# Attention's stores on GpSimd's queue, fewer loads for the scan, and the block solve in four half slots

## The chip, the cores and the metric

The kernel runs on one core of one Trainium2 chip. The metric is device time in microseconds (us) of one execution. The engines are named as the profile names them: PE (TensorE, the matmuls), PEld (its weight loads), DVE (VectorE), ACT (ScalarE), POOL (GpSimd) and SP (SyncE, which here only issues DMAs). A "queue" is the list of DMAs that one engine issues: SPq, ACTq, POOLq. An engine issues its own DMAs in its own instruction stream, so a DMA that has to wait holds up what stands behind it on that engine.

## The reference

One inference step of a two-layer hybrid backbone, for 128 context tokens and 1024 latent tokens of width 1024. In every layer the modulated input goes through one input projection whose columns feed three heads side by side; their outputs are joined, projected and normalised, and a gated feed-forward part follows:

```
z_rw, zq, zkv, zkr, zu, zv = split_proj(x * (1 + scale1) + shift1, w_in, rw_conv)
y_rw, s_fin = rwkv7_bidir(z_rw, s0)     # 4 heads of 64, forward and backward over the tokens:
      S = S * w_t + (S @ -kk_t) (kk_t * a_t)^T + v_t k_t^T ;  out_t = S @ r_t
y_mla = attend(...)                     # 8 heads: softmax(scale * (q_nope k_nope + q_rope k_rope)) @ v,
                                        # 1024 latent queries over 1152 keys, 128 context queries over 128
y_gm  = chunk_mlp(zu, zv)
x = layer_norm(ALPHA * x + gate1 * (concat(y_rw, y_mla, y_gm) @ w_out))
x = layer_norm(ALPHA * x + gate2 * swiglu(x * (1 + scale2) + shift2))
```

All of it is float32 in and out. The outputs are the two token streams, the compressed attention caches and the final scan states of the context.

## The kernel before

**Stages.** Each layer runs the input projection, the preparation of attention's q, k and v (written to DRAM as `qd`, `kd`, `vd`) and of the scan's inputs (decays `sd`, columns `zd`, values `vtd`), then one stage in which attention and the RWKV scan are woven together, then `w_out` and the feed-forward part. A matmul of float32 accuracy is written as three products of split operands, lines L119 to L121. Only the woven stage matters here. It runs in layer 0 from about 365 to 920 us and in layer 1 from about 2250 to 2797 us.

**Weaving.** `rwkv` (L891) drives `mla` (L717), which is a generator called `other`. Inside `manual_schedule` (L954) the order of the code is the order of the instructions on PE, DVE, ACT, POOL and SP. `slot(first, work)` (L931) does: the next piece of attention (scores, exponentials and maxima, the *scores half*), then the actions of `first`, then the next piece of attention (the products with the values, the *products half*), then the actions of `work`. Attention has 16 units (8 heads by two sets of queries) of 5 slots, 80 slots in all. At the start of a unit ACT issues the loads of its `kT` (L786) and `qT` (L729). The maximum of each query row is found one unit ahead: PE computes scores (L735), DVE takes maxima (L740, L746, L748 into `eye`), PE transposes them (L753) and ACT writes them into `qT` (L754). ACT's exponentials `P` are L762, POOL adds them up in `acc` (L847), DVE takes the reciprocal `rc` (L777), POOL multiplies `o` (L778), and ACT stores `o` to `yd` (L782), 40 DMAs in a layer.

**The scan's pipeline.** The scan has 9 segments of 128 tokens (one of context, eight of latents), in both directions. A step `i` of the loop has six slots, k0 to k5; it scans segment i while the later segments are prepared by `flow[i+1]`, `flow[i+2]` and `flow[i+3]` (`rw_operands` L982, `rw_solve` L1071, `rw_double` L1128). Steps i=-2 to 8 take 66 slots, 7 more finish the last blocks, and attention's last 7 slots follow alone. For one segment:

- three steps ahead: k0 the loads `szin` and `zin`, two each (SP, L994 and L996); k1 the loads `UV` (L1003); k2, in `first`, the set-up: ACT's exponentials of `szin` (L1016, L1018, L1021) and POOL's product with `zin` (L1022); k3 and k4 the products on DVE and POOL (L1030 to L1035);
- two steps ahead: k0 and k1 the pair matrix `M1` (L1052, L1055, L1056); k2 stores to DRAM (L1067, L1082); k3 the load `Db` of its diagonal blocks (L1085); then the *solve* on DVE, a doubling in sizes s = 2, 4, 8, each with two halves x = 0 and 1 (a product L1113 and a sum L1114): s = 2 and 4 in k4, s = 8 in k5, with a copy (L1118) and two stores to `xbd` (SP, L1120);
- one step ahead: k0 the loads `xz` of that result, four DMAs (SP, L1125), in `work`, behind `szin` and `zin` of the other segment; k2 to k5 the larger doubling on PE, which begins with `Q` from `xz` (L1140).

After a block of the scan is done, `rw_post` normalises it through `po_y` and `po_t` (L1243 to L1279) and stores it; `po_y` has two buffers.

**DMA completion.** DMAs of SP and of ACT share counters ("lanes"): the trace shows an ACT load or store that begins only when an earlier DMA of SP has landed, though neither needs the other's data.

Of the kernel before, what the change touches and what calls it, by code (L numbers as in the profile page):

```python
# [8 lines left out]
F32 = mybir.dt.float32  # L9
# [10 lines left out]
T_LAT, T_CTX = 1024, 128  # L20
T = T_LAT + T_CTX
# [10 lines left out]
C = 64  # L32
# [46 lines left out]
class Net:  # L79
# [304 lines left out]
    def project_cols(self, l, tmp, tmp2):  # L384

        nc = self.nc
        where = [ZR[0], ZR[1], ZK[0], ZK[1], ZV[0], ZV[1], None, None, ZG]
        rows = (slice(0, 64), slice(64, 128))
# [10 lines left out]
        def decay(m, zc):  # L399

            for d in range(2):
                for ct in range(2):
                    x = self.t(tmp, [128, T], "kk", bufs=2)
                    for b in range(NB):
                        p = self.psum("bg")
                        nc.tensor.matmul(p[:, 0:BLK], lora[m][rows[d], 128 * ct:128 * ct + 128], zc[rows[d], b * BLK:b * BLK + BLK], start=True, stop=True)  # L406
                        o = x[:, b * BLK:b * BLK + BLK] if d == 0 else x[:, T - b * BLK - BLK:T - b * BLK][:, ::-1]
                        i = 4 * (m - 6) + 2 * d + ct
                        nc.scalar.activation(o, p[:, 0:BLK], AF.Tanh, scale=0.5, bias=hv[:, i:i + 1])
                    if m == 6:  # L410
                        nc.vector.tensor_scalar(x, x, 0.5, 0.5, op0=ALU.mult, op1=ALU.add)
                        y = self.t(tmp, [128, T], "kk", bufs=2)
                        for b in range(NB):
                            bs = slice(b * BLK, b * BLK + BLK)
                            nc.vector.tensor_tensor_scan(y[:, bs], smask, x[:, bs], 0.0, op0=ALU.mult, op1=ALU.add)
                        x = y
                    else:
                        nc.gpsimd.tensor_scalar(x, x, -0.5, -0.5, op0=ALU.mult, op1=ALU.add)
                    nc.scalar.dma_start(self.sd[:, d, 2 * (m - 6) + ct], x)

        def values(ct, zc):

# [14 lines left out]
        for mp in (2, 3, 1, 0, 4):  # L437
            n = 256 if mp < 4 else 128
            wh, wl = self.w_in_chunk(l, 256 * mp, n)
            for mi in range(n // 128):  # L440
                m = 2 * mp + mi
                z = self.t(tmp, [128, T + 3], "zraw", bufs=2)
# [4 lines left out]
                for b in range(NB):  # L447
                    p = self.psum("ps")
# [8 lines left out]
                w = [self.v(l, "rw_conv", 9 * i + m) for i in range(3)]  # L457
# [16 lines left out]
                if m in (2, 3):  # L474
# [3 lines left out]
                    p = self.psum("bg")  # L478
# [238 lines left out]
    def mla(self, l, ap):  # L717

        nc = self.nc
# [44 lines left out]
        def finish(h, q0, nq, po, acc):  # L764

            w = min(nq, 256)
            parts = range(nq // w)
            r = slice(0, 64 * len(parts))
            o = self.t(ap, [128, 256], "o", bufs=2)
            nc.scalar.copy(o[r, 0:w], po[r, 0:w])  # L770

            yield
            p = self.psum("as")
            for i in parts:
                nc.tensor.matmul(p[64 * i:64 * i + 64, 0:w], ones, acc[:, w * i:w * i + w], start=True, stop=True)
            rc = self.t(ap, [128, 256], "rc")
            nc.vector.reciprocal(rc[r, 0:w], p[r, 0:w])  # L777
            nc.gpsimd.tensor_tensor(o[r, 0:w], rc[r, 0:w], o[r, 0:w], op=ALU.mult)  # L778
            yield
            c = slice(64 * (h % 2), 64 * (h % 2) + 64)  # L780
            for i in parts:
                nc.scalar.dma_start(self.yd[c, 2 + h // 2, q0 + w * i:q0 + w * i + w], o[64 * i:64 * i + 64, 0:w])  # L782

        def head(h):
            kT = k_tiles[h % 2]
# [13 lines left out]
        q_tiles = {x: [self.t(ap, [NQR, 2, nq], f"qT{x}{i}", F32R) for i in range(n)] for x, nq, n in (("", 512, 3), ("c", 128, 2))}  # L799
        k_tiles = [self.t(ap, [NQR, 2, NK], f"kT{i}", F32R) for i in range(2)]  # L800
        for n, t in enumerate([k_tiles[0], q_tiles[""][0], q_tiles[""][1], q_tiles["c"][0], k_tiles[1], q_tiles[""][2], q_tiles["c"][1]]):
            (nc.gpsimd if n % 2 else nc.vector).memset(t[96:128].bitcast(F32), 0.0)
        for t in k_tiles:
            nc.vector.memset(t[96:97, 0].bitcast(F32), 1.0)
            nc.sync.dma_start(t[64:96].bitcast(F32), self.krd)

        units = [(h, q) for h in range(8) for q in ([0], [T_LAT, 512])]
# [82 lines left out]

    def rwkv(self, l, rp, other):  # L891
        nc = self.nc
        g2 = self.t(rp, [128, 256], "rg2")
        nc.gpsimd.dma_start(g2, self.I["rw_g2"][l])
        hv = self.t(rp, [128, 4], "rhv")
# [33 lines left out]
        def turn(g):  # L929
            return lambda: next(g, None)  # L930
# [16 lines left out]
            nc.sync.dma_start(self.O["o_state"][0, l].rearrange("d h v k -> v (d h) k"), so.rearrange("p (a k) -> p a k", k=64))  # L947
        for _ in range(6):
            next(flow[0])
        next(other)  # L950

        E = mybir.EngineType
        with self.tc.manual_schedule(engines={E.PE, E.DVE, E.Activation, E.Pool, E.SP}):
            post, posts = [], []  # L954
            for i in range(-2, n):
                scan = self.rw_scan(segs[i], rp, Y, state, **kept[i]) if i >= 0 else iter(())
                ends = [turn(p) for p in posts]
                posts = [self.rw_post(l, b, rp, Y, g2, brk) for b in post]
                post = []
                for k in range(6):  # L960
                    first, work = [turn(p) for p in posts], [turn(scan)]
                    if 0 <= i + 2 < n:
                        work.append(turn(flow[i + 2]))
                    if 0 <= i + 3 < n:
                        (first if k == 2 else work).append(turn(flow[i + 3]))
                    if 0 <= i + 1 < n and k != 1:
                        (first if k > 1 else work).append(turn(flow[i + 1]))
                    if (i, k) == (1, 2):
                        first.insert(0, end_of_context)
                    slot(first, work + (ends if k == 0 else []))  # L970
                if i == 0:
                    post.append(8)
                if i >= 5:
                    post += [8 - i, i - 1]
            ends = [turn(p) for p in posts]
            posts = [self.rw_post(l, b, rp, Y, g2, brk) for b in post]
            for k in range(7):
                slot([], [turn(p) for p in posts] + (ends if k == 0 else []))

    def rw_operands(self, seg, rp, hv, Q, Xb, xd, kept):  # L980
# [6 lines left out]
        cc = lambda a: a.rearrange("p (j c) t -> p c j t", j=2)  # L987
        UV = self.t(rp, [128, 2, 2, 4, 64], "UV", bufs=4)
        zs, vs, stores = [], [], []
        for d in range(2):  # L990
            lo = t0 if d == 0 else T - f0 - n
            tn, fn = slice(lo, lo + n), slice(t0, t0 + n) if d == 0 else slice(f0, f0 + n)
            sz = self.t(rp, [128, 4, 128], "szin", bufs=2)
            nc.sync.dma_start(sz, self.sd[:, d, :, fn])  # L994
            z = self.t(rp, [128, 6, 128], "zin", bufs=2)
            nc.sync.dma_start(z, self.zd[:, 0:6, tn])  # L996
            zs.append((tn, z, sz))
            vs.append(fn.start // C)
        yield

        for d in range(2):
            for h in range(2):
                nc.sync.dma_start(UV[rows[h], h, d], self.vtd[d, h, :, vs[d]:vs[d] + 2].rearrange("p j c v -> p (j c) v"))  # L1003
        yield
        AR, BK = {}, {}
        EP = self.t(rp, [128, 2, 4], "EP", bufs=4)
# [64 lines left out]
    def rw_solve(self, rp, M1, Xb, xd, kept):  # L1071
# [22 lines left out]
        for s in (2, 4, 8):  # L1094
            b = 8 // s
            q = self.t(rp, [64, 64], "Xq")
            for x in range(2):
                pr = self.t(rp, [64, 512], "pr_x")

                if x == 0:  # L1100
                    l, m = (D, s, 34 * s, 1, 0, 16), (X, 0, 34 * s, 0, 1, 16)
                    o = q[:, 0:s * s * b]
                else:
                    l, m = (X, 17 * s, 34 * s, 16, 0, 1), (q, 0, s * s, 0, 1, s)
                    o = at(X, 16 * s, (34 * s, b), (16, s), (1, s))

                def part(a, o, sb, si, sj, sk):

                    if s == 2:
                        return [at(a, o + j * sj, (sb, b), (si, s), (sk, s)) for j in range(s)]  # L1110
                    return [at(a, o + i * sb, (si, s), (sj, s), (sk, s)) for i in range(b)]
                for p_, l_, m_ in zip(part(pr, 0, s ** 3, s * s, s, 1), part(*l), part(*m)):
                    nc.vector.tensor_tensor(p_, l_, m_, op=ALU.mult)  # L1113
                nc.vector.tensor_reduce(o, pr[:, 0:s ** 3 * b].rearrange("p (a k) -> p a k", k=s), axis=AX.X, op=ALU.add)  # L1114
            if s == 4:
                yield
        Xs, Xt = (Xb[:, x].rearrange("p (a b) -> p a b", a=16) for x in range(2))
        nc.vector.tensor_copy(Xt, Xs.rearrange("p a b -> p b a"))  # L1118
        for x, y in enumerate((Xs, Xt)):
# [106 lines left out]
    def rw_post(self, l, b, rp, Y, g2, brk):  # L1226
# [13 lines left out]
        def tmp(tag):  # L1240
            return self.t(rp, [128, 2, 128], tag, bufs=2)
        p = bank()
        nc.tensor.matmul(p, self.bones, y, start=True, stop=True)  # L1243
        yc = tmp("po_y")
        nc.vector.scalar_tensor_tensor(yc, p, -1.0 / 64, y, op0=ALU.mult, op1=ALU.add)
        sq = tmp("po_t")
        nc.scalar.activation(sq, yc, AF.Square)
# [414 lines left out]
```

## Time and profile before

| | |
|---|---|
| median of 3 runs | 3781.65 us (3773.04 to 3784.24) |
| the profiled execution | 3778.69 us, of which the span is 3776.9 us |
| PE, DVE, ACT, POOL busy | 93%, 50%, 29%, 36% of the span |
| mean granted clock of PE | 0.957 |

A row of a window gives its length, then busy time and instruction count of PE, PEld, DVE, ACT and POOL, the granted clock as a share of the full 2.4 GHz (0.50 is 1.2 GHz), the share of DMA time and GB/s. A row of a timeline gives start, duration, engine (with q: its queue), line, operation, tiles, count, and in brackets the idle time before it and what ended it.

### The profile page before, as it was taken

Reading aid. Unit: us, or ns where it says so; the run is one execution under the profiler, and the core shown is the slowest. Engines: PE = TensorE matmul, PEld = TensorE weight load, DVE = VectorE, ACT = ScalarE, POOL = GpSimd, SP = SyncE. Lnnn points to the kernel's source line nnn. Section 1 sums busy time; section 2 is a strip of 40 time slices with the busy share of each in tenths; the row PEclk is TensorE's granted clock in tenths of the full one; section 3 lists DMA queues with packets and bytes.
Section 4 is the critical chain, followed back from the end, with each engine's and each line's share of the span. In section 5 each row is a group of like instructions: output and inputs, shape, how many; then the busy total and the mean of one; then the engine's idle time right before and its main releaser. Section 6 shows DMA issues by size and latency. Waiting matters only on the chain.

```text
span 3776.9 us, 61399 instructions
## 1 busy us (share of the span) xinstructions
PE 3519.4 (93%) x25199; PEld 3048.4 (81%) x25199; DVE 1883.6 (50%) x3076; ACT 1098.7 (29%) x2156; POOL 1372.8 (36%) x1223
## 2 busy tenths in 40 slices
PE   8998788888999999999999988888998999999996
PEld 6888566666988888988988885666778999999995
DVE  3545665655733333333455465566559333333356
ACT  3443444423421111111144434343333311111111
POOL 2322656644511111111543237556445111111145
PEclk9999788999999999999999998899999999999998
DMA  7566545434332222221325565444343111111122
GB/s 288 158 220 164 114 100 104 96 77 149 107 107 78 90 79 78 67 67 56 107 103 143 192 147 109 99 97 88 78 159 107 51 45 45 39 40 45 45 84 78
DMA packets 466137, 387.13 MB, mean 102 GB/s; under 512 B 171148, under 2 KB 398856, under 8 KB 464640
## 3 DMA queue, kind: packets, MB, share of 16 engines
q1 hardware_dynamic: 372608, 249.12, 23.7%
q10 hardware_dynamic: 87424, 118.42, 10.4%
q0 software_dynamic: 5824, 15.66, 1.3%
q8 instruction: 198, 3.24, 0.4%
q14 instruction: 83, 0.68, 0.1%
HBM read 280.10 MB, written 103.02 MB: 101 GB/s over the span
## 4 chain that ended last, share of the span: by engine, by line
PE 74%; DVE 12%; DMA 6%; issue 2%; ACT 2%; POOL 1%; SPq 1%; ACTq 0%; POOLq 0%; DVEq 0%
PE b L119 19%; PE b L121 18%; PE b L120 18%; PE b L867 3%; DVE pr_x L1113 2%; PE b L355 2%; PE b L242 2%; DMA xz<-xbd 2%; DVE mx L740 1%; PE b L735 1%; PE b L406 1%; DVE hyl L126 1%; PE b L1140 1%; DMA zin<-zd 1%; DVE rc L777 1%
## 5 line engine op out<-in xcount | busy, mean ns | idle before, releaser
L121 PE MATMUL b<-hyh,w 128*128 128x384 f32 x2544 | 858.8, 338 | 1.4 <-DVE w L319 1.4
L119 PE MATMUL b<-hyh,w 128*128 128x384 f32 x2448 | 823.1, 336 | 0.0
L120 PE MATMUL b<-hyl,w 128*128 128x384 f32 x2448 | 821.9, 336 | 0.0
L319 POOL TENSOR_TENSOR w<-wr,w 128x2048 fp32r<-128x2048 f32 x64 | 296.9, 4640 | 1189.2 <-ACT w L316 989.0
L121 PEld LDWEIGHTS b<-hyh,w 128*128 128x128 f32 x2544 | 479.0, 188 | 26.3 <-issue 23.9
L119 PEld LDWEIGHTS b<-hyh,w 128*128 128x128 f32 x2448 | 460.1, 188 | 20.8 <-issue 19.4
L120 PEld LDWEIGHTS b<-hyl,w 128*128 128x128 f32 x2448 | 460.1, 188 | 9.7 <-issue 8.3
L1406 DVE TENSOR_TENSOR fs<-fs,b 128x384 f32<-128x384 f32 x132 | 72.9, 553 | 627.1 <-PE b L121 623.0
L847 POOL TENSOR_TENSOR acc<-acc,P 128x512 f32<-128x512 f32 x224 | 297.1, 1326 | 179.4 <-ACT P L762 169.9
L316 ACT CAST w<-wr 128x2048 fp32r<-128x2048 f32 (+2 forms) x86 | 161.2, 1874 | 583.8 <-PE b L120 511.9
L120 PE MATMUL b<-w,hidh 128*128 128x512 f32 x756 | 299.5, 396 | 0.0
L121 PE MATMUL b<-w,hidl 128*128 128x512 f32 x756 | 299.4, 396 | 0.0
L119 PE MATMUL b<-w,hidh 128*128 128x512 f32 x756 | 298.3, 396 | 0.0
L126 DVE TENSOR_TENSOR hidl<-fs,hidh 128x384 fp32r<-128x384 f32 x126 | 230.6, 1831 | 81.5 <-ACT hidh L125 79.5
L1420 DVE TENSOR_TENSOR acc<-acc,b 128x512 f32<-128x512 f32 x288 | 191.5, 684 | 139.0 <-PE b L121 139.0
L762 ACT ACTIVATE P<-b 128x512 f32<-128x512 f32 x288 | 169.7, 600 | 207.8 <-PE b L121 176.8
L740 DVE TENSOR_REDUCE mx<-b 128x1 f32<-128x512 f32 x256 | 169.0, 682 | 120.2 <-PE b L735 119.4
L867 PE MATMUL b<-P,vt 128*64 128x256 f32 x1152 | 180.1, 432 | 3.9 <-ACT P L762 3.2
L119 PE MATMUL b<-w,hyh 128*128 128x256 f32 x576 | 167.0, 292 | 16.9 <-ACT hyh L125 5.4
L125 ACT CAST hidh<-fs 128x384 fp32r<-128x384 f32 x126 | 64.4, 512 | 396.4 <-DVE fs L1406 396.4
L119 PE MATMUL b<-qT,kT 128*128 128x512 f32 x288 | 138.4, 480 | 38.3 <-DVE mx L740 30.0
L1405 ACT ACTIVATE fs<-b 128x384 f32<-128x384 f32 x132 | 64.8, 493 | 372.5 <-PE b L121 362.2
(437 smaller groups left out, 6953.1 us busy)
## 6 DMA issues: line engine op xcount, KB each, us to landing
wr<-in_ffn_w_in_dram SPq DMA_DIRECT2D x88, 512.0 KB, 4.7
fx<-in_ada_w_dram SPq DMA_DIRECT2D x28, 1024.0 KB, 5.1
wr<-in_ffn_w_out_dram SPq DMA_DIRECT2D x22, 1024.0 KB, 4.8
wr<-in_ada_w_dram SPq DMA_DIRECT2D x20, 1024.0 KB, 8.8
qT<-qd ACTq DMA_DIRECT2D x32, 448.0 KB, 6.3
zin<-zd SPq DMA_DIRECT2D x36, 384.0 KB, 5.3
xres<-x ACTq DMA_DIRECT2D x27, 512.0 KB, 3.6
wr<-in_w_in_dram SPq DMA_DIRECT2D x12, 1024.0 KB, 6.2
```

The lines of the kernel that those rows point to most:

```text
L119: mm(out, ah, bh, start=(i == 0), stop=False)
L120: mm(out, ah, bl, start=False, stop=False)
L121: mm(out, al, bh, start=False, stop=(i == n - 1))
L126: (lo_eng or self.nc.vector).tensor_tensor(lo, src, hi.bitcast(F32), op=ALU.subtract)
L242: nc.tensor.matmul(p[32 * jj:32 * jj + 32, :], self.sc[:, 2 * jj + e, :], w[:, 2 * j + e, :], start=(e == 0), stop=(e == 1), tile_position ...
L316: self.nc.scalar.copy(hi, r)
L319: (eng or self.nc.gpsimd).tensor_tensor(lo[:, s], r[:, s], hi[:, s].bitcast(F32), op=ALU.subtract)
L740: nc.vector.tensor_reduce(mx[:, i, c:c + 1], p, axis=AX.X, op=ALU.max)
L762: nc.scalar.activation(P[:, 0:nq], p[:, 0:nq], AF.Exp, scale=MLA_SCALE)
L847: nc.gpsimd.tensor_tensor(acc, Ps[0] if k == 1 else acc, P, op=ALU.add)
L867: nc.tensor.matmul(po[0][64 * i:64 * i + 64, 0:256], vt[:, k], Ps[k][:, 256 * i:256 * i + 256], start=(k == 0), stop=(k == 9))
L1420: nc.vector.tensor_tensor(acc[i][:, w], acc[i][:, w], p, op=ALU.add)
```

## The change

1. **Stores.** Attention's stores of `o` (L782) go from ACT's queue to POOL's.
2. **Loads.** The two `szin` loads of a segment become one DMA, the four `UV` loads become two. For this the decays of the second direction are stored in DRAM in turned order, which takes 4 DMAs more in a layer, in the projection stage.
3. **Order of loads.** The `xz` loads stand in k0's `first`, so ahead of `szin` and `zin` on SP; the `Db` load stands in k3's `first`.
4. **Solve.** Its four parts take four half slots: s = 2 in k4's `first`, s = 4 in k4's `work`, s = 8 with x = 0 in k5's `first`, s = 8 with x = 1, the copy and the stores in k5's `work`.
5. **Start.** Attention's prologue (`next(other)`, with the first maxima) moves to the head of `rwkv`, all the zeroing of its `qT` and `kT` goes to POOL, and two slots of attention alone come ahead of step i=-2, so that 75 slots hold the scan and 5 follow.
6. `po_y` gets four buffers.

```diff
-                nc.scalar.dma_start(self.yd[c, 2 + h // 2, q0 + w * i:q0 + w * i + w], o[64 * i:64 * i + 64, 0:w])
+                nc.gpsimd.dma_start(self.yd[c, 2 + h // 2, q0 + w * i:q0 + w * i + w], o[64 * i:64 * i + 64, 0:w])
...
-            (nc.gpsimd if n % 2 else nc.vector).memset(t[96:128].bitcast(F32), 0.0)
+            nc.gpsimd.memset(t[96:128].bitcast(F32), 0.0)
...
     def rwkv(self, l, rp, other):
         nc = self.nc
+        next(other)
...
-        next(other)
...
             post, posts = [], []
+            for _ in range(2):
+                slot([], [])
...
                     if 0 <= i + 2 < n:
-                        work.append(turn(flow[i + 2]))
+                        for part in (first, work) if k > 3 else (first if k == 3 else work,):
+                            part.append(turn(flow[i + 2]))
                     if 0 <= i + 3 < n:
                         (first if k == 2 else work).append(turn(flow[i + 3]))
                     if 0 <= i + 1 < n and k != 1:
-                        (first if k > 1 else work).append(turn(flow[i + 1]))
+                        first.append(turn(flow[i + 1]))
...
+        szs = self.t(rp, [128, 2, 4, 128], "szin")
+        nc.sync.dma_start(szs.rearrange("p d a t -> p (d a) t"), self.sd[:, :, :, t0:t0 + n].rearrange("p d a t -> p (d a) t"))
...
-            sz = self.t(rp, [128, 4, 128], "szin", bufs=2)
-            nc.sync.dma_start(sz, self.sd[:, d, :, fn])
...
-            if s == 4:
-                yield
+                if s == 8 and x == 0 or s < 8 and x == 1:
+                    yield
...
-        yc = tmp("po_y")
+        yc = self.t(rp, [128, 2, 128], "po_y", bufs=4)
```

On SP, at the end of k5 and in k0 of step i=1, before (`xbd` is the solve's result, `po_rk` and `po_v` are loads for a finished block, `xz` the same result loaded back):

```order
L1120 DMA xbd_464_2861<-Xb_3666 64x16x16 x2
L1233 DMA po_rk_5074<-rkd_76 128x4x128
L1234 DMA po_v_5075<-zd_69 128x3x128
L994 DMA szin_5116<-sd_70 128x4x128
L996 DMA zin_5118<-zd_69 128x6x128
L994 DMA szin_5120<-sd_70 128x4x128
L996 DMA zin_5122<-zd_69 128x6x128
L1125 DMA xz_5124<-xbd_464_2861 64x8x64 x4
```

The same place now:

```order
L1131 DMA xbd_464_2865<-Xb_3738 64x16x16 x2
L1244 DMA po_rk_5122<-rkd_76 128x4x128
L1245 DMA po_v_5123<-zd_69 128x3x128
L1136 DMA xz_5126<-xbd_464_2865 64x8x64 x4
L1002 DMA szin_5173<-sd_70 128x8x128
L1007 DMA zin_5175<-zd_69 128x6x128
L1007 DMA zin_5177<-zd_69 128x6x128
```

`xz` has moved ahead of the three loads of the other segment, which were four.

On DVE, in k5 of one step and the beginning of the next k0, before (`mx` and `eye` are attention's maxima, `pr_x` to `Xb` the solve with s = 8, `St` and `S` the scan's state):

```order
L740 TENSOR_REDUCE mx_5192<-b_973_5546 128x1
L740 TENSOR_REDUCE mx_5192<-b_976_5556 128x1
L1277 TENSOR_TENSOR po_y_5153<-po_y_5153,b_977_5559 128x256
L1208 TENSOR_TENSOR St_5613<-b_979_5587,S_5308 128x256
L1209 TENSOR_TENSOR S_5612<-St_5613,EP_3929 128x256
L1113 TENSOR_TENSOR pr_x_5619<-Db_5432,Xb_3666 64x512
L1114 TENSOR_REDUCE Xq_5618<-pr_x_5619 64x64
L1113 TENSOR_TENSOR pr_x_5622<-Xb_3666,Xq_5618 64x512
L1114 TENSOR_REDUCE Xb_3666<-pr_x_5622 64x8x8
L1118 COPY Xb_3666<-Xb_3666 64x256
L740 TENSOR_REDUCE mx_5192<-b_989_5641 128x1
L740 TENSOR_REDUCE mx_5192<-b_990_5644 128x1
```

The same place now:

```order
L747 TENSOR_REDUCE mx_5094<-b_981_5576 128x1
L747 TENSOR_REDUCE mx_5094<-b_984_5586 128x1
L753 TENSOR_REDUCE mx_5094<-b_985_5589 128x4
L755 TENSOR_REDUCE eye_3660<-mx_5094 128x4
L1288 TENSOR_TENSOR po_y_5203<-po_y_5203,b_986_5596 128x256
L1124 TENSOR_TENSOR pr_x_5601<-Db_5413,Xb_3738 64x512
L1125 TENSOR_REDUCE Xq_5600<-pr_x_5601 64x64
L1219 TENSOR_TENSOR St_5653<-b_991_5627,S_5356 128x256
L1220 TENSOR_TENSOR S_5652<-St_5653,EP_3985 128x256
L1124 TENSOR_TENSOR pr_x_5658<-Xb_3738,Xq_5600 64x512
L1125 TENSOR_REDUCE Xb_3738<-pr_x_5658 64x8x8
L1129 COPY Xb_3738<-Xb_3738 64x256
```

The first half of s = 8 has moved ahead of the scan's state; all four solve instructions still stand ahead of the next slot's maxima.

On ACT, at the start of the stage of layer 0, before (`PB`, `pr_i`, `pr_k` are the set-up of one direction, `qT0` takes the first maxima, `P` are the first exponentials):

```order
L1016 ACTIVATE PB0_557_3696<-szin_550_3681 128x2x2x64
L1018 ACTIVATE pr_i_558_3699<-szin_550_3681 128x256
L1021 ACTIVATE pr_k_559_3701<-szin_550_3681,rhv_541_3658 128x128 x2
L754 ACTIVATE qT0_571_3740<-b1_588_3792 1x512
L1016 ACTIVATE PB1_560_3705<-szin_552_3685 128x2x2x64
L1018 ACTIVATE pr_i_561_3708<-szin_552_3685 128x256
L1021 ACTIVATE pr_k_562_3710<-szin_552_3685,rhv_541_3658 128x128 x2
L762 ACTIVATE P_594_3810<-b2_595_3811 128x512
```

The same place now:

```order
L1027 ACTIVATE PB0_579_3764<-szin_573_3753 128x2x2x64
L1029 ACTIVATE pr_i_580_3767<-szin_573_3753 128x256
L1032 ACTIVATE pr_k_581_3769<-szin_573_3753,rhv_564_3730 128x128 x2
L1027 ACTIVATE PB1_582_3773<-szin_573_3753 128x2x2x64
L1029 ACTIVATE pr_i_583_3776<-szin_573_3753 128x256
L1032 ACTIVATE pr_k_584_3778<-szin_573_3753,rhv_564_3730 128x128 x2
L761 ACTIVATE qT0_542_3664<-b1_559_3716 1x512
L769 ACTIVATE P_593_3810<-b2_594_3811 128x512
```

Both directions of the set-up now stand ahead of `qT0`, which the first scores need.

## Rows read from the trace of the kernel before

**Rows 1.** Window over the nine steps i=-1 to 7, layer 0.

```profile
419.70:811.70 392.00, 334.70 (x4390) 256.38 (x4390) 234.78 (x440) 150.28 (x346) 223.14 (x236) 0.89 0.45 96
```

**Rows 2.** Waits of PE, 330 to 930 us: total, times, longest in us.

```profile
PE b L119 <- DVE mx L740: 14.3, 8, 4.4
PE b L735 <- ACT P L762: 12.7, 5, 5.9
PE b L1140 <- DMA xz<-xbd: 9.9, 7, 3.5
PE b L1252 <- ACT po_t L1247: 6.7, 1, 6.7
```

**Rows 3.** Windows, the nine k2 slots: two of layer 0, sums of layers 0 and 1.

```profile
513.20:529.00 15.80, 10.44 (x125) 8.96 (x122) 3.89 (x9) 5.57 (x15) 6.67 (x9) 0.78 1.02 213
...
610.40:617.30 6.90, 6.78 (x116) 5.53 (x114) 3.47 (x7) 4.98 (x13) 6.82 (x8) 1.00 0.86 160
...
sum 102.90, PE 74.47 PEld 59.60 DVE 25.34 ACT 41.57 POOL 63.96; mean PE 8.27 PEld 6.62 DVE 2.82 ACT 4.62 POOL 7.11
...
sum 107.00, PE 76.64 PEld 61.88 DVE 25.31 ACT 41.70 POOL 63.80; mean PE 8.52 PEld 6.88 DVE 2.81 ACT 4.63 POOL 7.09
```

**Rows 4.** Timelines of ACT and PE inside three long k2 slots, layer 0.

```profile
437.08 1.07 ACT L1055 COPY M<-b 128x512 f32<-128x512 f32 x2 [7.96 <-DMA xz<-xbd]
...
438.71 0.48 PE L735 MATMUL b<-kT,qTc 128*128 128x128 f32 x1 [5.92 <-ACT P L762]
...
520.07 1.08 ACT L762 ACTIVATE P<-b 128x512 f32<-128x512 f32 x2 [5.65 <-DMA zin<-zd]
...
783.68 1.87 PE L1252 MATMUL b<-cst,po_t 128*128 128x2 f32 x8 [6.70 <-ACT po_t L1247]
```

**Rows 5.** Timeline of SP's queue, one k5 and k0 (step i=3, layer 0).

```profile
599.46 1.29 SPq L1120 DMA_DIRECT2D xbd<-Xb  x2
600.81 0.65 SPq L994 DMA_DIRECT2D szin<-sd  x1
...
604.99 3.22 SPq L1125 DMA_DIRECT2D xz<-xbd  x4
```

**Rows 6.** DMA issues, 365 to 930 us: count, KB each, median us to landing.

```profile
xz<-xbd SPq DMA_DIRECT2D x36, 128.0 KB, 5.4
szin<-sd SPq DMA_DIRECT2D x18, 256.0 KB, 4.4
...
yd<-o ACTq DMA_DIRECT2D x32, 64.0 KB, 2.1
...
xbd<-Xb SPq DMA_DIRECT2D x18, 64.0 KB, 2.6
...
so<-in_state_rwkv_dram POOLq DMA_DIRECT2D x2, 64.0 KB, 5.7
```

**Rows 7.** Timeline of ACT: the set-up in k2 of step i=3.

```profile
612.89 0.41 ACT L1016 ACTIVATE PB<-szin 128x256 f32<-128x256 f32 x1
...
614.88 0.87 ACT L1021 ACTIVATE pr_k<-szin,rhv 128x128 f32<-128x128 f32 x2
```

**Rows 8.** Windows, the nine k0 slots of layer 0: one of them, and the sum.

```profile
712.80:724.00 11.20, 5.73 (x68) 4.09 (x66) 10.96 (x20) 2.64 (x5) 9.68 (x9) 1.00 0.01 2
...
sum 80.80, PE 59.23 PEld 41.70 DVE 75.70 ACT 17.94 POOL 47.05; mean PE 6.58 PEld 4.63 DVE 8.41 ACT 1.99 POOL 5.23
```

**Rows 9.** Timeline of ACT at the stage's start, layer 0.

```profile
382.76 0.42 ACT L1016 ACTIVATE PB<-szin 128x256 f32<-128x256 f32 x1
...
384.27 0.59 ACT L754 ACTIVATE qT<-b 1x512 fp32r<-1x512 f32 x1
```

**Rows 10.** Timeline of PE, two slots of attention alone, layer 0.

```profile
869.89 0.50 PE L119 MATMUL b<-qT,kT 128*128 128x512 f32 x1
...
872.49 0.50 PE L119 MATMUL b<-qT,kT 128*128 128x512 f32 x1
```

**Rows 11.** Window over the end of the stage, layer 0.

```profile
870.00:920.00 50.00, 37.73 (x204) 25.14 (x205) 28.27 (x34) 22.73 (x42) 27.37 (x32) 0.83 0.54 173
```

**Rows 12.** Groups of POOL, 365 to 930 us: the price of issuing a DMA there.

```profile
L912 POOL DMA_DIRECT2D so<-in_state_rwkv_dram x2 | 1.3, 633 | 0.0
```

More of the change, by code (lines that the diff above doesn't have):

```diff
@@ L133, in copy, with both @@
             self.nc.vector.tensor_copy(out, in_)
+    def both(self, a, b):
+        assert [list(x) for x in a.ap] == [list(x) for x in b.ap]
+        return bass.AP(a.tensor, a.offset, [a.ap[0], [b.offset - a.offset, 2], *a.ap[1:]])
     def rsqrt(self, out, in_, n):
@@ L418, in decay @@
                         nc.gpsimd.tensor_scalar(x, x, -0.5, -0.5, op0=ALU.mult, op1=ALU.add)
-                    nc.scalar.dma_start(self.sd[:, d, 2 * (m - 6) + ct], x)
+                    for a, e, o in [(0, T, 0)] if d == 0 else [(0, T_CTX, T_LAT), (T_CTX, T, 0)]:
+                        nc.scalar.dma_start(self.sd[:, d, 2 * (m - 6) + ct, o:o + e - a], x[:, a:e])
         def values(ct, zc):
@@ L801, in mla @@
         for n, t in enumerate([k_tiles[0], q_tiles[""][0], q_tiles[""][1], q_tiles["c"][0], k_tiles[1], q_tiles[""][2], q_tiles["c"][1]]):
-            (nc.gpsimd if n % 2 else nc.vector).memset(t[96:128].bitcast(F32), 0.0)
+            nc.gpsimd.memset(t[96:128].bitcast(F32), 0.0)
         for t in k_tiles:
-            nc.vector.memset(t[96:97, 0].bitcast(F32), 1.0)
+            nc.gpsimd.memset(t[96:97, 0].bitcast(F32), 1.0)
             nc.sync.dma_start(t[64:96].bitcast(F32), self.krd)
@@ L989, in rw_operands @@
         zs, vs, stores = [], [], []
+        szs = self.t(rp, [128, 2, 4, 128], "szin")
+        nc.sync.dma_start(szs.rearrange("p d a t -> p (d a) t"), self.sd[:, :, :, t0:t0 + n].rearrange("p d a t -> p (d a) t"))
         for d in range(2):
             lo = t0 if d == 0 else T - f0 - n
-            tn, fn = slice(lo, lo + n), slice(t0, t0 + n) if d == 0 else slice(f0, f0 + n)
-            sz = self.t(rp, [128, 4, 128], "szin", bufs=2)
-            nc.sync.dma_start(sz, self.sd[:, d, :, fn])
+            tn = slice(lo, lo + n)
             z = self.t(rp, [128, 6, 128], "zin", bufs=2)
             nc.sync.dma_start(z, self.zd[:, 0:6, tn])
-            zs.append((tn, z, sz))
-            vs.append(fn.start // C)
+            zs.append((tn, z, szs[:, d]))
+            vs.append((t0 if d == 0 else f0) // C)
         yield
-        for d in range(2):
-            for h in range(2):
-                nc.sync.dma_start(UV[rows[h], h, d], self.vtd[d, h, :, vs[d]:vs[d] + 2].rearrange("p j c v -> p (j c) v"))
+        for h in range(2):
+            v = [self.vtd[d, h, :, vs[d]:vs[d] + 2].rearrange("p j c v -> p (j c v)") for d in range(2)]
+            nc.sync.dma_start(UV[rows[h], h].rearrange("p d a v -> p d (a v)"), self.both(*v))
         yield
```

## Prediction

> **What bounds the kernel now.** I read the windows first. PE is busy 93% of the span, but less in the woven stage: over the nine steps i=-1 to 7 of layer 0, 392.0 us or 43.6 us a step, PE works 334.7 us and its granted clock is 0.89, while DVE works 234.8 and POOL 223.1 us [rows 1]. So the stage is bound by nothing in the mean and by waits in turn; the list of PE's waits says which [rows 2]: DVE's maxima, ACT's `P`, the landing of `xz`, and once `po_t`. The same windows slot by slot put them in two places. The nine k2 slots take 102.9 us in layer 0 and 107.0 us in layer 1, though an undisturbed one takes 6.9 us; a stalled one takes 15.8 [rows 3]. The nine k0 slots of layer 0 take 80.8 us with PE busy 59.2 and DVE 75.7 [rows 8]. The reader should see that k2 is waiting for transfers and k0 for DVE: in k2 DVE is busy 25 of 103 us, in k0 it has no gaps to give.
>
> **k2, edits 1, 2, 3 and 6.** If every k2 slot took 6.9 us, nine would take 62 us: the excess is 41 us in layer 0 and 45 us in layer 1, 86 us together, with the time at half clock after each stall inside it. The timelines name three causes [rows 4]. (a) ACT stands 7.96 us until `xz` has landed; the instruction ahead of it is a store of `o`, which needs a counter that `xz` holds, and PE waits 5.92 us for the `P` behind it. With the stores on POOL this goes. (b) In another step ACT's `P` come 5.65 us late because its loads of `kT` and `qT` wait for `zin`; these loads stay on ACT. (c) PE waits 6.70 us for `po_t`, which waits for a buffer of `po_y` to be stored; four buffers take that away. In the remaining steps PE waits for `xz` itself, 9.9 us in all [rows 2].
>
> For `xz` I work out one step [rows 5]. The solve's stores are issued from 599.46 us and end at 600.75; `xz` is issued from 604.99, since four loads, one of them issued slowly, lie between, and takes 3.22 us to issue. Now SP waits for the stores to land (2.6 us by the median [rows 6]), so `xz` starts at about 603, 2 us earlier, and `szin` and `zin` no longer run ahead of it: its 5.4 us to landing [rows 6] should come down towards the 2.6 of a small load. That is 2 + 2.8, some 4 to 5 us earlier, against a longest wait for `xz` of 3.5 us [rows 2]. So (a), (c) and the `xz` waits go, and (b) stays in part: I take three quarters of 86, **-64 us**. The ends are all of it, -86, and what (a) and (c) alone are worth, 5.92 and 6.70 us of waiting in each layer and a microsecond of half clock behind each, -30.
>
> What is late next there is the set-up, since `szin` and `zin` are now issued behind `xz`. They are issued some 5.5 us later than before (2.6 for the stores, 3.2 for `xz`, against 0.1). ACT began the set-up at 612.89 [rows 7]; the issue of `szin` was over before 604.99 [rows 5], and with 4.4 us to landing [rows 6] it was there by about 609. So some 4 us of slack were there; the move uses them up and 1 to 2 us more, and ACT, busy 41.6 of 103 us in k2 [rows 3], can catch that up before the next slot's exponentials. I price this at nothing and keep the loss as a rival.
>
> **k0, edits 3 and 4.** The cover of k0 is DVE's own queue: in the longest slot shown DVE works 10.96 of 11.20 us while PE works 5.73 [rows 8]. The four half slots move no work off DVE, and in the order on DVE all of s = 8 still stands ahead of the next slot's maxima. Only an earlier start could help: the `Db` load and s = 2 come half a slot sooner, where DVE happens to be idle. I take about half a microsecond a step, **-8 us** for 18 steps; the ends are 0 and -40, PE's whole idle time of 21.6 us in these slots, for two layers.
>
> **The start, edit 5.** ACT's order now has both directions of the set-up ahead of `qT0`. One direction takes 384.27 - 382.76 = 1.5 us [rows 9], so the first scores come 1.5 us later, although the maxima are taken earlier. Two slots of attention alone take 2.6 us each [rows 10], and the scan starts behind them: 1.5 + 5.2 = 6.7 us in each layer, **+13 us**; the ends are +3 (DVE, freed of the zeroing, and less waiting in step i=-2) and +17. **The end.** Those two slots are gone from the end, 5.2 us a layer if PE sets the time there. But PE works only 37.7 of the 50 us after the scan, at clock 0.83 [rows 11]: it waits for the scan's output and the weights of `w_out`. I take **-6 us** for two layers; the ends are -10 and +6.
>
> **POOL, edit 1.** A DMA costs POOL 633 ns to issue [rows 12], so 40 stores take 25 us of POOL in a layer. POOL works 223 of 392 us [rows 1], so most of it is covered; in an undisturbed k2 it is not, since POOL works 6.82 of 6.9 us there [rows 3]. About 5 of the 40 stores fall in k2 slots, 3 us a layer if each pushes PE. I take **+2 us**; the ends are 0 and, with no cover at all, +50. ACT's issue time saved and SP's three fewer DMAs a segment lie beside PE's work: 0. The stores of the decays, 4 DMAs more in a layer, lie in a stage where I saw PE wait for no store: 0 to +2.
>
> A rule speaks against this edit. What the rows show: 64 KB on POOL's queue took 5.7 us to landing, the same size on ACT's 2.1 [rows 6], though the former is a load with short rows at a crowded moment. The Trainium skill, page "SBUF — State Buffer", section "SBUF: two separate sides", says that a DMA of GpSimd's queue has its descriptors written by GpSimd, which VectorE can lock out, so that the transfer stands still until VectorE's instruction ends; it advises ACT or SP. The row agrees in direction and doesn't prove it. By that rule a store would land 3.6 us later; nobody waits for a store but the reuse of `o` and the load for `w_out` at the end, so the sum would be at most 7 us higher. If the rule held POOL itself, that is the rival on POOL below.
>
> **The sum.** -64 - 8 + 13 - 6 + 2 = -63 us. The profiled execution took 3778.69 us, so 3716 us. It lies 3.0 us under the median of the runs, less than what a measurement of this kernel can tell from no change, about 0.3% or 11 us.
>
> **Rivals.**
> - *k0 takes back what k2 gives.* If DVE's solve is late whatever k2 does, PE reaches k0 earlier and waits there longer. For it: DVE 75.7 of 80.8 us in k0 [rows 8]. Against it: DVE is busy only 60% of a step [rows 1] and a quarter of k2 [rows 3], so it starts each solve without a backlog. Half of the 64 comes back: 3748 us.
> - *More than k2.* If the earlier start of the solve lets the maxima through in most steps, k0 gives 40 and not 8, and less half clock with it: 3716 - 37 = 3679 us. For it: PE's idle time in k0 is there to be had. Against it: the order on DVE.
> - *POOL becomes the bound.* All 50 us of issuing come to lie on the path, for instance because VectorE holds POOL up: 3716 - 2 + 50 = 3764 us. For it: POOL in k2. Against it: 43% idle over a step.
> - *It doesn't do what it says.* The maxima are not ahead of the set-up where it counts (ACT, above), and if `xz` still lands late because four small loads queue behind others, only (a) and (c) go, and the start and the end are at their upper ends: 3778.7 - 30 + 17 + 6 + 2 = 3774 us, within 0.3%.
> - *Slower: the set-up waits for `szin`.* ACT's set-up stands ahead of the exponentials of the next slot. Seven of nine k2 slots in a layer hold one, 14 in all. Each microsecond by which `szin` comes too late for the path costs 14 us. It decides from 63 / 14 = 4.5 us on; at 6 us late, as with an `xz` that takes 6 us to issue and a load of 512 KB that lands in 7, it is +84 - 63 = +21: 3800 us. For it: the slack is used up [rows 5, 7]. Against it: ACT's idle time in k2 [rows 3] and a transfer that is one DMA less.
>
> **How the numbers follow.** My forecast, 3690 to 3735, 0.45; more than k2, 0.15; k0 takes back, 0.18; POOL, 0.05; no effect, 0.08; slower, 0.09. Faster by over 0.3% (under 3767) holds the first three and half of POOL: 0.81. Within 0.3%: 0.10. Slower: 0.09. The range runs from all of k2 with a good part of k0 (-86 - 30 + 10 - 10 = -116, 3662) to the weakest sum (3774); it leaves out the slower case, part of no effect and a tail of the best case, some 0.18.
>
> **What the changed profile would show.** Right: no wait of ACT for `xz` or of PE for `po_t`, PE's wait for `xz` under 3 us a layer, k2 slots near 7 us with one or two still long behind ACT's loads; k0 slots hardly changed; first scores 1 to 2 us later and the scan's first step 6 to 7 us later; the end of the stage shifted by as much as the scan's end. Wrong: ACT's first set-up instruction waiting for `szin` in most k2 slots (the slower case), PE waiting for `acc` or `P` behind POOL's stores, or PE's wait for `mx` up by 15 us or more in each layer (k0 takes back).

## The result, and the profile after

The changed kernel takes 3722.8 us (median of 4 runs, 3713.69 to 3730.89) against 3782.94 us for the kernel before (4 runs, 3773.04 to 3789.73): a ratio of 0.9851, 95% interval 0.983 to 0.9871, some 56 us faster. The forecast was 3716 us, 3662 to 3774. Its profiled execution took 3724.55 us with a span of 3722.8 us, 54.1 us less than the span before.

The nine steps of each layer first, which answer [rows 1]. Columns as there.

```profile
422.80:787.60 364.80, 325.26 (x4393) 249.68 (x4391) 251.47 (x445) 150.19 (x348) 241.87 (x266) 0.92 0.50 108
2272.10:2642.00 369.90, 327.07 (x4394) 251.57 (x4392) 245.02 (x445) 150.22 (x348) 241.89 (x266) 0.91 0.48 106
```

Layer 0 went from 392.0 to 364.8 us; PE's idle time and its half clock shrank together, 0.89 to 0.92. Layer 1 had 395.6 us before. Nearly all of the gain lies in these steps, some 27 and 26 us.

PE's waits, 330 to 930 us, answer [rows 2].

```profile
PE b L119 <- ACT w L321: 15.7, 2, 14.1
PE b L742 <- DVE mx L747: 9.4, 5, 2.5
PE b L119 <- DVE mx L747: 7.8, 8, 2.7
PE b L742 <- ACT P L769: 7.6, 6, 2.2
...
PE b L119 <- ACT qT L761: 6.8, 1, 6.8
...
PE b L1151 <- DMA xz<-xbd: 1.5, 3, 1.0
```

`xz` is down from 9.9 to 1.5 us, `po_t` is gone, the longest wait for `P` is 2.2 and not 5.9. New in layer 0 is the wait for the weights of `w_out` at the stage's end, and the one for `qT` at its start is longer. SP's queue at the place of [rows 5], and the DMA issues of 365 to 930 us (these answer [rows 6]):

```profile
589.45 1.49 SPq L1131 DMA_DIRECT2D xbd<-Xb  x2
591.96 2.63 SPq L1136 DMA_DIRECT2D xz<-xbd  x4
```

```profile
xz<-xbd SPq DMA_DIRECT2D x36, 128.0 KB, 5.2
...
yd<-o POOLq DMA_DIRECT2D x32, 64.0 KB, 2.0
```

SP issues `xz` 2.5 us behind the solve's stores and no longer 5.5. In this step it lands 3.0 us after its issue instead of 6.9, but by the median of the layer hardly sooner than before, 5.2 and 5.4 us. The sums of the nine k2 slots, layers 0 and 1, answer [rows 3]:

```profile
sum 65.60, PE 61.70 PEld 51.17 DVE 24.55 ACT 33.14 POOL 51.26; mean PE 6.86 PEld 5.69 DVE 2.73 ACT 3.68 POOL 5.70
sum 63.60, PE 60.23 PEld 49.90 DVE 24.66 ACT 29.67 POOL 51.75; mean PE 6.69 PEld 5.54 DVE 2.74 ACT 3.30 POOL 5.75
```

k2 gave 37.3 and 43.4 us, 81 together. Part of it went into the slot behind it. The nine k3 slots, layer 0 before, then layers 0 and 1 after:

```profile
sum 59.20, PE 58.48 PEld 47.49 DVE 37.03 ACT 21.53 POOL 25.05; mean PE 6.50 PEld 5.28 DVE 4.11 ACT 2.39 POOL 2.78
```

```profile
sum 65.30, PE 60.29 PEld 48.29 DVE 44.14 ACT 26.97 POOL 39.22; mean PE 6.70 PEld 5.37 DVE 4.90 ACT 3.00 POOL 4.36
sum 74.00, PE 64.35 PEld 51.93 DVE 44.49 ACT 30.24 POOL 40.27; mean PE 7.15 PEld 5.77 DVE 4.94 ACT 3.36 POOL 4.47
```

Layer 1 had 59.3 us before, so k3 took back 6 and 15 us. The nine k0 slots answer [rows 8], layers 0 and 1:

```profile
sum 82.70, PE 62.84 PEld 44.33 DVE 72.97 ACT 16.89 POOL 46.70; mean PE 6.98 PEld 4.93 DVE 8.11 ACT 1.88 POOL 5.19
sum 82.80, PE 61.22 PEld 43.00 DVE 72.83 ACT 16.66 POOL 45.55; mean PE 6.80 PEld 4.78 DVE 8.09 ACT 1.85 POOL 5.06
```

They were 80.8 and 79.8: no gain there, a loss of 2 or 3 us. What k3's products need is ACT's set-up. Its waits, 330 to 930 us, and one of them in the timeline (this answers [rows 7]):

```profile
ACT PB L1027 <- DMA szin<-sd: 12.5, 5, 3.1
```

```profile
600.19 0.42 ACT L1027 ACTIVATE PB<-szin 128x256 f32<-128x256 f32 x1 [2.74 <-DMA szin<-sd]
```

In layer 1 it waits 14.1 us, also five times. Before, ACT's set-up waited for `szin` only at the stage's start. The start itself, ACT and PE (this answers [rows 9]):

```profile
384.81 0.42 ACT L1027 ACTIVATE PB<-szin 128x256 f32<-128x256 f32 x1
...
387.71 0.59 ACT L761 ACTIVATE qT<-b 1x512 fp32r<-1x512 f32 x1
...
388.35 0.80 PE L119 MATMUL b<-qT,kT 128*128 128x512 f32 x1 [6.83 <-ACT qT L761]
```

And PE at the end of layer 0's stage:

```profile
861.94 0.58 PE L119 MATMUL b<-w,hyh 128*128 128x256 f32 x1 [14.06 <-ACT w L321]
```

### The profile page after: what moved, and what is told of

Same layout as the page of the kernel before. It is cut to its first block, busy times and chain, and to the rows that moved or that the text cites. A ratio compares the mean times of both kernels' runs of the same rounds, so it can differ in the third digit from the quotient of the medians.

```text
span 3722.8 us, 61377 instructions
## 1 busy us (share of the span) xinstructions
PE 3494.9 (94%) x25199; PEld 3033.4 (81%) x25199; DVE 1896.9 (51%) x3064; ACT 1096.9 (29%) x2156; POOL 1430.2 (38%) x1315
## 4 chain that ended last, share of the span: by engine, by line
PE 74%; DVE 11%; DMA 6%; issue 3%; ACT 3%; POOL 2%; SPq 1%; ACTq 0%; POOLq 0%; DVEq 0%
PE b L119 19%; PE b L121 19%; PE b L120 19%; PE b L874 2%; PE b L360 2%; PE b L247 2%; DVE pr_x L1124 2%; DMA szin<-sd 1%; PE b L742 1%; PE b L411 1%; DVE mx L747 1%; PE b L1063 1%; DVE hyl L126 1%; DMA wr<-in_w_out_dram 1%; DMA wr<-in_w_in_dram 1%
## 5 line engine op out<-in xcount | busy, mean ns | idle before, releaser
L747 DVE TENSOR_REDUCE mx<-b 128x1 f32<-128x512 f32 x256 | 169.3, 683 | 106.3 <-PE b L742 105.4
L742 PE MATMUL b<-kT,qT 128*128 128x512 f32 (+1 forms) x384 | 125.1, 385 | 49.7 <-DVE mx L747 19.0
```

Of the source, the lines that this page charges most:

```text
L742: nc.tensor.matmul(p[:, 0:n], qT[0][:, 128 * i:128 * i + 128], kT[0][:, k0:k0 + n], start=True, stop=True)
L747: nc.vector.tensor_reduce(mx[:, i, c:c + 1], p, axis=AX.X, op=ALU.max)
```

## The experiments

The theory to be tested: the gain is the place of `xz` and the two further buffers of `po_y`; a part was given back because the set-up now waits for `szin`; the solve, the stores and the start are worth about nothing. Each kernel was timed against the kernel before, and the ratios are to that; the changed kernel's is 0.9851. Where a part is undone, the name of the run begins with u. No run takes out edit 2 alone, or the earlier `Db` load of edit 3: what these are worth by themselves is not shown.

**u_xz, the place of the `xz` loads.**

```diff
-                        first.append(turn(flow[i + 1]))
+                        (first if k else work).append(turn(flow[i + 1]))
```

> The changed kernel with the xz loads back behind szin and zin (k0's work). Theory A (xz's place is what freed k2): PE's wait for xz returns to 8 to 13 us a layer, k2 slots grow by 15 to 20 us a layer and k3 slots shrink by 5 to 10, since szin is early again: about 3740 to 3748 us. Rival B (what xz gains the late set-up takes back): within 6 us of the changed kernel.

3765.27 us, 0.9952 (0.9935 to 0.9969): 38 us of the gain are gone, more than theory A gave. The k2 sums of layers 0 and 1, and PE's wait for `xz` in layer 0:

```profile
sum 93.80, PE 71.31 PEld 57.83 DVE 24.78 ACT 40.77 POOL 63.99; mean PE 7.92 PEld 6.43 DVE 2.75 ACT 4.53 POOL 7.11
sum 97.50, PE 74.23 PEld 60.71 DVE 25.63 ACT 40.89 POOL 64.90; mean PE 8.25 PEld 6.75 DVE 2.85 ACT 4.54 POOL 7.21
```

```profile
PE b L1151 <- DMA xz<-xbd: 10.3, 8, 4.1
```

k2 grew by 28 and 34 us, while ACT no longer waits for `szin` in any step and k3 fell back to 59.3 and 59.2. So the place of `xz` is the largest part, and the price of it is seen in k3.

**u_poy, two buffers of `po_y`.**

```diff
-        yc = self.t(rp, [128, 2, 128], "po_y", bufs=4)
+        yc = self.t(rp, [128, 2, 128], "po_y", bufs=2)
```

> The changed kernel with two po_y buffers again. Theory: PE waits about 6.7 us for po_t once in each layer, in k2 of step i=7, with a microsecond or two of half clock behind it: slower by 10 to 17 us, about 3736 us. Rival (the scan has slack there, or the wait is hidden since the store of po_y is issued sooner): within 5 us.

3742.51 us, 0.9899 (0.9885 to 0.9913): 18 us, a little over what was expected. The k2 slot of step i=7 is 16.1 us long again (9.6 in the changed kernel), in layer 1 17.1 (10.6), and DVE's waits name the store:

```profile
763.80:779.90 16.10, 10.66 (x110) 8.88 (x106) 3.00 (x8) 2.46 (x6) 6.21 (x8) 0.68 0.32 69
```

```profile
DVE po_y L1256 <- DMA yd<-po_y: 6.7, 1, 6.7
```

**u_solve, the solve in two pieces.** The `yield`s and the slots go back, the `Db` load stays in k3's `first`.

```diff
-                        for part in (first, work) if k > 3 else (first if k == 3 else work,):
+                        for part in (first if k == 3 else work,):
...
-                if s == 8 and x == 0 or s < 8 and x == 1:
-                    yield
+            if s == 4:
+                yield
```

> The changed kernel with the solve in two pieces again (s = 2 and 4 in k4's work, s = 8 in k5's work). Theory (DVE has the same work ahead of the next maxima either way): within 6 us of the changed kernel, k0 slots at 80 to 84 us a layer. Rival (the half slots let the maxima and the reciprocals through): slower by 10 to 20 us, k0 or k5 slots longer by 5 to 10 us a layer.

3735.87 us, 0.9878 (0.9861 to 0.9896): 10 us slower than the changed kernel, though the two intervals still overlap. The time is the rival's. The k0 sums of layers 0 and 1, and PE's waits for the maxima in layer 0:

```profile
sum 89.50, PE 61.22 PEld 43.43 DVE 80.81 ACT 17.24 POOL 48.95; mean PE 6.80 PEld 4.83 DVE 8.98 ACT 1.92 POOL 5.44
sum 86.10, PE 56.20 PEld 39.77 DVE 79.01 ACT 17.50 POOL 48.73; mean PE 6.25 PEld 4.42 DVE 8.78 ACT 1.94 POOL 5.41
```

```profile
PE b L742 <- DVE mx L747: 19.7, 5, 5.5
PE b L119 <- DVE mx L747: 14.1, 8, 3.4
```

DVE has 6 to 8 us more to do inside k0 with the solve in two pieces: the half slots put that work earlier, and k0 is 7 and 3 us shorter for it. That alone is not the gain, since the nine k5 slots are 3 and 5 us longer in the changed kernel (59.2 and 58.5 against 56.2 and 53.3). The waits side with the rival: those two for the maxima took 17.2 us in the changed kernel and take 33.8 here, so the half slots let the maxima through.

**u_start and u_slots, edit 5.** u_start undoes all of it, u_slots takes out only the two slots:

```diff
-            for _ in range(2):
-                slot([], [])
```

> The changed kernel without the two slots ahead, with the prologue and the zeroing where they were before. Theory (a shift: the scan starts some 7 us sooner, step i=-2 gets longer by about as much, the end hardly moves): within 8 us of the changed kernel. Rival (starting later pushes the end of the stage out by the whole 5 to 7 us a layer): faster by 10 to 14 us.

> The changed kernel without the two slots ahead, but with the prologue still at the head and the zeroing on POOL; with edit 5 wholly undone it took 3710.5 us. Theory (the two slots shift attention's units against the scan's steps, so that more maxima meet the solve in k0): k0 slots at 72 to 75 us a layer, 3705 to 3715 us. Rival (the loss lies in the prologue's place, which moves work at the end of the projection stage): k0 stays near 82 us, 3718 to 3728 us.

u_start took 3710.5 us, 0.9814 (0.9797 to 0.9831), u_slots 3709.88 us, 0.9821 (0.9808 to 0.9833). Edit 5 is a loss of 11 to 14 us (the intervals just touch that of the changed kernel), and the two slots are all of it that can be measured. The time is that of u_start's rival, the reason that of u_slots' theory: the k0 sums of u_start are

```profile
sum 74.10, PE 55.98 PEld 38.29 DVE 70.47 ACT 17.46 POOL 42.26; mean PE 6.22 PEld 4.25 DVE 7.83 ACT 1.94 POOL 4.70
sum 72.60, PE 55.48 PEld 38.40 DVE 68.25 ACT 17.48 POOL 43.18; mean PE 6.16 PEld 4.27 DVE 7.58 ACT 1.94 POOL 4.80
```

9 and 10 us a layer below the changed kernel's, with 2 to 5 us less of DVE's work in them, and u_slots shows the like, 69.9 and 73.6 us. A unit has 5 slots and a step 6, so two slots more move every unit's maxima and reciprocals against the solve. In this alignment more of the maxima meet it in k0: in layer 0 DVE spends 13.6 us on their first reductions (L747) inside the nine k0 slots, in u_slots 10.1. Of the reciprocals that isn't so: PE waits 6.8 us for them in layer 0 of the changed kernel and 9.2 in u_slots.

**szin_first and szin_early, the set-up's load.** In szin_first `szin` stands between the solve's stores and `xz`, in szin_early in k5 ahead of the stores (the generator yields between `szin` and `zin`; `zin` stays behind `xz`). The main lines of szin_early:

```diff
...
+                    if k == 5 and 0 <= i + 4 < n:
+                        first.insert(0, turn(flow[i + 4]))
...
```

> The changed kernel with the one szin load issued right behind the solve's stores, in the time in which SP waits for these to land, so ahead of xz; the two zin loads stay behind xz. Theory A (k3 grew by 6 and 15 us because ACT's set-up waits for szin): the set-up starts without a wait, k3 slots fall back towards 60 us a layer, xz lands at most 1 to 2 us later: faster by 8 to 20 us, about 3709 us. Rival B (k3 grew because DVE and POOL are late there, whatever szin does): k3 unchanged, within 5 us of the changed kernel or slower through xz.

> The changed kernel with the szin load issued in k5 ahead of the solve's stores, and zin behind xz. Theory A (late szin makes k3 longer): as with szin_first, faster by 8 to 20 us, and xz not delayed at all. Rival B (zin on POOL and DVE, or DVE itself, makes k3 longer): within 5 us of the changed kernel.

szin_first: 3721.56 us, 0.9847 (0.9829 to 0.9866), nothing in the time where theory A wanted 8 to 20 us. szin_early: 3706.51 us, 0.9798 (0.9782 to 0.9813), 20 us faster than the changed kernel. The sums of szin_first, k3 in layers 0 and 1, then k2:

```profile
sum 60.40, PE 58.85 PEld 47.43 DVE 41.09 ACT 21.23 POOL 40.73; mean PE 6.54 PEld 5.27 DVE 4.57 ACT 2.36 POOL 4.53
sum 59.40, PE 57.94 PEld 46.87 DVE 39.40 ACT 21.13 POOL 38.52; mean PE 6.44 PEld 5.21 DVE 4.38 ACT 2.35 POOL 4.28
...
sum 69.60, PE 61.34 PEld 50.74 DVE 24.62 ACT 40.68 POOL 53.88; mean PE 6.82 PEld 5.64 DVE 2.74 ACT 4.52 POOL 5.99
sum 81.20, PE 68.17 PEld 55.85 DVE 24.91 ACT 40.54 POOL 58.11; mean PE 7.57 PEld 6.21 DVE 2.77 ACT 4.50 POOL 6.46
```

and of szin_early, k3:

```profile
sum 61.00, PE 59.42 PEld 47.87 DVE 40.59 ACT 21.31 POOL 42.37; mean PE 6.60 PEld 5.32 DVE 4.51 ACT 2.37 POOL 4.71
sum 59.40, PE 58.15 PEld 46.86 DVE 40.61 ACT 20.51 POOL 39.30; mean PE 6.46 PEld 5.21 DVE 4.51 ACT 2.28 POOL 4.37
```

In both, k3 is back at 59 to 61 us, so late `szin` is what made k3 longer. In szin_first the transfer runs ahead of `xz` and k2 gives it back, 4 and 18 us; in szin_early k2 stays at 64.4 and 63.3. So theory A holds for what made k3 longer, and the prices of the two places are seen apart. The profiled execution of szin_first was its longest, 3733.75 us, so the 18 us are that execution's and may be high.

**setup_work, the set-up half a slot later** (`flow[i + 3]` always in `work`).

> The changed kernel with the set-up in k2's work, behind attention's products, so half a slot later on ACT and POOL. Theory A (the set-up comes up before its data): POOL's acc and ACT's copies pass ahead of it; ACT's wait for szin of 12.5 us in layer 0 falls below 5 us; the time changes by -10 to 0 us. Rival B (what counts is when the set-up ends, as k3's products need it): slower by 5 to 15 us.

3745.13 us, 0.9903 (0.9886 to 0.9919): 20 us slower, beyond rival B. ACT's wait for `szin` in the steps is gone and k2 is about as short as in the changed kernel, 64.6 and 67.2 us, but the nine steps take 374.7 and 373.7 us against 364.8 and 369.9, with k3 at 72.6 and 73.0. In layer 0 that fits rival B: most of the growth, 7 of 10 us, lies in k3, whose products need the end of the set-up. In layer 1 it isn't shown, since k3 took 74.0 us in the changed kernel too and the growth of 4 us lies in k2.

**u_stores, b_stores and early_act, the stores.** u_stores is the changed kernel with the stores back on ACT, b_stores the kernel before with this edit alone, early_act the fastest kernel below with them back on ACT.

```diff
-                nc.gpsimd.dma_start(self.yd[c, 2 + h // 2, q0 + w * i:q0 + w * i + w], o[64 * i:64 * i + 64, 0:w])
+                nc.scalar.dma_start(self.yd[c, 2 + h // 2, q0 + w * i:q0 + w * i + w], o[64 * i:64 * i + 64, 0:w])
```

> The changed kernel with attention's stores back on ACT's queue, all else as changed (3722.8 us). Theory (the stores held ACT until xz had landed, POOL's 40 issues a layer are covered): slower by 10 to 25 us, about 3738 us, and ACT's exponentials or copies behind a store again wait several us for xz or szin in one or two k2 or k3 slots of each layer. Rival (POOL's issuing costs as much as ACT's waits did, 25 us of POOL in a layer): within 6 us of the changed kernel, or faster.

> The kernel before with one edit, attention's stores on POOL's queue. Theory (a store on ACT held the exponentials until xz had landed, 5.92 us of PE in k2 of step i=-1 in each layer, and less elsewhere): that wait is gone, k2 of step i=-1 falls from 13.2 towards 9 us, 8 to 16 us faster, 3767 to 3775 us. Rival (PE then waits for xz itself in the same slot, and POOL is late by its issues): within 5 us of before.

> The fastest kernel so far (szin ahead of the solve's stores, edit 5 undone: 3690.25 us, ratio to before 0.9766) with attention's stores back on ACT's queue. It settles what edit 1 is worth once xz and szin are early; with it undone in the changed kernel the ratio was 0.9863 against 0.9851, with overlapping intervals, and alone on the kernel before it was worth nothing. Theory A (a store on ACT still waits there for transfers of SP): slower by 8 to 20 us, ratio 0.979 to 0.982. Theory B (with xz and szin early, ACT's stores find their counters free, and POOL saves 25 us of issuing a layer): within 5 us, or faster.

u_stores: 3731.01 us, 0.9863 (0.9847 to 0.9879), some 5 us and inconclusive against 0.9851, short of the theory's 10 to 25. b_stores: 3782.49 us, 1.0004 (0.9992 to 1.0015), nothing, where the theory wanted 8 to 16. early_act: 3685.68 us, 0.9754 (0.9737 to 0.977), against 0.9766 (0.9754 to 0.9779) with them on POOL: nothing either. In b_stores the slot of [rows 4]'s first wait is as short as the theory said, and PE's wait for `xz` is longer:

```profile
428.60:436.40 7.80, 5.12 (x67) 3.86 (x65) 2.01 (x4) 4.93 (x12) 7.68 (x8) 1.00 1.16 244
```

```profile
PE b L1140 <- DMA xz<-xbd: 13.0, 10, 4.1
```

That slot gave 5.4 us, all nine of layer 0 only 3.7 (102.9 to 99.2), and the k1 slots took 2.6 of them. With `xz` late the wait moved on to it. With `xz` early ACT's stores meet it seldom: in layer 0 ACT waits for `xz` once, 1.8 us in u_stores and 2.2 in early_act, against 8.0 in the kernel before. The edit removes a wait that the place of `xz` removes too.

**early_start, the two best together:** szin_early with edit 5 undone.

> The changed kernel with szin issued in k5 ahead of the solve's stores and with edit 5 undone (no slots ahead, prologue and zeroing where they were before), the two edits that each gave a ratio to before of 0.980 and 0.981 alone, against 0.985 for the changed kernel. Theory (they act in different places, k3 and the start with the alignment of k0): both gains add, ratio 0.976, about 3690 us. Rival (both shorten the same waits): no better than one of them, 3703 to 3710 us.

3690.25 us, 0.9766 (0.9754 to 0.9779): the gains add. Its k0 sums are 73.6 and 75.1, its k3 sums 61.6 and 61.3. With early_act these are the fastest kernels here, 2.3 to 2.5% below the kernel before and some 1% below the changed one.

## Why the prediction was right, and where its steps failed

The sum was -63 us, the profiled spans differ by 54 and the medians by 60. The undone parts add up: 38 (`xz`), 18 (`po_y`), 10 (solve), 5 (stores, unclear) and -14 (edit 5), 57 us in all. Each was undone by itself, so that they add up to the whole is no proof that they don't overlap. By its steps:

- **k2, -64: right in kind, too small.** It gave 81 us. Three quarters were taken because ACT's loads of `kT` and `qT` stay on ACT; with `xz` early they wait less too. The working for `xz` was right in its step and not in the mean: the 2.6 us it was to land in are those of a 64 KB store, while `xz` is four loads of 128 KB, and over the layer their 5.4 us became 5.2. What came earlier is the issue, 2.5 to 2.7 us behind the solve's stores in seven of the nine steps of layer 0, before 3.7 to 5.8. Not right was the part of cause (a): the stores' wait was real, but b_stores shows that taking it away alone is worth nothing.
- **The set-up at nothing: the step that failed.** Its slack was read rightly, some 4 us against a move of 5.5, but not that ACT could catch it up. ACT waited for `szin` five times in layer 0, 12.5 us, and k3 grew by 21 us in two layers. Five of the seven set-ups in each layer waited, so one of the named signs of being wrong was there. It is the "slower" rival in a mild form, mostly 2 to 3 us late and not 6; szin_early gives the 20 us back.
- **k0, -8: wrong in sign, by another edit.** The half slots are worth 3 to 7 us a layer in k0, as u_solve shows, though k5 takes 3 and 5 us back; "they move no work off DVE" missed that they move work out of k0 and let maxima pass. The two slots of edit 5 took 9 to 10 us a layer away again by moving attention's units against the steps. The prediction priced them as a delay and not as a shift of alignment.
- **The start, +13: too large.** The first scores came 3.4 us later (384.92 to 388.35), not 1.5: beside the second direction of the set-up, 1.4 us, the one `szin` load landed 2 us later than the first of two had. Neither comes from edit 5: in u_start ACT still does both directions ahead of `qT0`, and the first scores are no sooner (392.07). The one `szin` load of edit 2 is the likely cause; no run shows it alone. Step i=-2 began 10.5 us later in layer 0, but then took 27.4 and not 34.8 us, so that only 3.1 us were left at step i=-1. In layer 1 0.6 us were left there, measured from the feed-forward part of layer 0: some 4 us in two layers, close to the lower end that was named.
- **The end, -6: about 0.** Attention's last slot begins 33 us earlier in layer 0, the feed-forward part 25.6 us: PE waits 14.06 us at once for the weights of `w_out` in between. The prediction had named that wait from [rows 11], where PE's busy share alone is seen; here it is in the list. The nine steps had ended 24.1 us earlier, so the end itself gave 1.5 us in layer 0 and next to nothing in layer 1.
- **POOL, +2, and the rival on POOL:** no loss that can be measured, 0.9766 against 0.9754 with the stores on ACT. The rule that was weighed against the edit (the Trainium skill, page "SBUF — State Buffer", section "SBUF: two separate sides") would have made stores late. They landed in 2.0 us by the median, against 2.1 on ACT's queue before, so this case doesn't show it. The last section has the one place where DVE stood still.
- **"It doesn't do what it says"** held for the start alone: both directions of the set-up stand ahead of `qT0`, and PE waits 6.83 us for it.

So the total was right in part by luck, because errors of opposite sign met: k2 by 17 us too small against 21 us missing in k3, and a start 9 us too dear against a k0 13 us too cheap.

## What to carry to other kernels

A load that feeds the next step should be issued where its queue would only wait: `szin` behind `xz` and ahead of it both cost 20 us against the place half a slot before the stores. When two loops with periods of 5 and 6 slots are woven, a shift by two slots is no mere delay but another alignment of all their waits; price it by what meets what in each slot. A wait that is taken away is worth only what the next wait in the same slot leaves, so try the edit alone before it is counted.

## What the runs showed of the hardware

One instruction of DVE in layer 0 of the changed kernel, an elementwise product of two SBUF operands whose median is 0.43 us, took 6.78 us. POOL was busy for nearly all of that time. Timelines of DVE and POOL:

```profile
601.32 6.78 DVE L1220 TENSOR_TENSOR S<-St,EP 128x256 f32<-128x256 f32 x1
```

```profile
600.04 0.57 POOL L789 DMA_DIRECT2D yd<-o  x1
600.63 2.53 POOL L1067 TENSOR_TENSOR M<-M,cst 128x512 f32<-128x512 f32 x2
603.12 1.27 POOL L854 TENSOR_TENSOR acc<-acc,P 128x512 f32<-128x512 f32 x1
...
607.14 0.67 POOL L1042 TENSOR_TENSOR AR<-zin,PB 128x256 f32<-128x256 f32 x1
```

From `M` on POOL did ten operations on end, the last of which ended at 607.8 us; DVE's instruction ended at 608.1. The same instruction took 2.8 to 6.9 us once in each layer of the eight kernels with POOL's stores, the solve in four half slots and `xz` ahead of `zin`, and at most 1.5 us in the kernel before, u_stores, early_act, b_stores, u_xz and u_solve. The Trainium skill, page "SBUF — State Buffer", section "SBUF: two separate sides", says that GpSimd and a VectorE instruction with two SBUF inputs exclude each other for the length of an instruction; here DVE seems to have been kept out for a whole row of POOL's instructions. That is argued from the timeline: no run took POOL's row of instructions apart. What it costs isn't settled either: in that k3 slot, 9.7 us long, PE was still busy 8.3 us; in u_stores, which has no long instruction, the same slot took 10.8 us; and szin_early has the same long instruction with k3 back at 61 us.
